# Layer 0's input projection computed by Strassen's seven block products instead of eight

## The chip, the cores and the metric

One core of a Trainium2 chip runs the whole program. The metric is the device time of one execution in microseconds (us). Three runs of the kernel before gave 2211.99, 2215.3 and 2217.59 us, a median of 2215.3 us.

## What is computed

The program is one inference step of a two-layer decoder trunk, for a prompt of 2048 tokens and 64 sample tokens (8 sequences of 8) that share the weights. Layer 0 runs a pooling mixer and a differential attention behind one joint input projection; layer 1 is gated linear attention (GLA). The change concerns the input projection of layer 0 and what uses its result:

```python
def even_layer(x, pos0, layer_idx, pool_buf, k_past, v_past,
               w_in, w_pool_lin, pool_scale, lam, subln_w, w_out, ln_g, ln_b):
    b, t, _ = x.shape
    pu, pg, q, k, v, ag = jnp.split(x @ w_in, EVEN_SPLITS, axis=-1)
    pool_out, new_buf = pool_mixer(pu, pool_buf, pos0, w_pool_lin, pool_scale)
    ...
    q = rope_partial(q.reshape(b, t, DA_HEADS, 2, DA_QK_DIM), pos) * DA_QK_DIM ** -0.5
    k = rope_partial(k.reshape(b, t, DA_HEADS, 2, DA_QK_DIM), pos)
    ...
    mix = jnp.concatenate([pool_out * jax.nn.silu(pg), o * jax.nn.silu(ag)], axis=-1)
    y = layer_norm(DN_ALPHA * x + mix @ w_out, ln_g, ln_b)
```

Here x has 2112 rows of 1024 and w_in has 3072 columns, six blocks of 512: the pool input pu and its gate pg, queries q, keys k, values v and the attention's gate ag. The pool mixer takes, for each of 4 groups of 128 channels, the mean over the last 2, 4, 8 or 16 tokens minus the token, maps it by a 128x128 matrix and scales it.

## The kernel before, in words

Every fp32 operand of the projection is cut in two: a high part (a cast to the fp32r type) and a low part (the raw value minus the high part). `split` (L39) does it: the cast on ScalarE (ACT, L42) or VectorE (DVE, L46), the subtraction on DVE (L47). A product is then three matmuls, high by high, high by low and low by high (`mm3`, L53 to L55), added up in one bank of PSUM.

`project_even` (L254) works in two halves. The first half is feature-major: the 2048 columns of queries, keys, pool inputs and pool gates are 16 blocks of 128, taken in 8 pairs by `fm_pair` (L274). A pair runs over five chunks of tokens (512, 512, 512, 256 and 320, the last with the 64 sample tokens), and each chunk is 8 slices of the contraction by 3 matmuls for each of its two blocks. In these matmuls (named pm<-xh,wh and so on) a 128x128 piece of the weights stands still and 512 tokens stream. The first pair is the rotated part of queries and keys (`rope_sink`), then four pairs of a pool group and its gate (`pool_sink`), then three pairs that are only copied out.

For a chunk of a pool group, ACT copies the input out of PSUM (ut, L349) and takes the gate's SiLU (sg, L352). DVE builds the trailing sums in one to four doublings (wp, L335), subtracts the token (dd, L355; the first 16 tokens anew, L358 and L359), cuts dd into dh and dl (L46, L47); TensorE (PE) multiplies by the group's matrix with three small matmuls (pl); DVE scales that and multiplies the gate (mx, L376). The two banks of the pool `pl` hold nothing but these products. While DVE does this for one chunk, PE does the 48 matmuls of the next.

The second half is token-major: for the gates (L427) and then the values (L440) 128 tokens stand still and 512 columns stream (pt<-wh,xh), 24 matmuls per tile of 128 tokens, 16 tiles, and one tile for the sample tokens. GpSimd (POOL) multiplies the gate by a weight (L428) and issues its store (L429). Among the last value tiles `layers` (L175) issues the first steps of the attention (`units`), and after that the attention's first head is woven with the pool half of the output projection (`out_pool`, names zp).

Weights come through a queue of SyncE (SP) as units of 128x1024 (L143), in raw buffers of which there are four, and are cut into four places for pairs of high and low parts (L144). All of x stays in SBUF as high and low parts (`XSplit`). A scheduler sets the order of the instructions on each engine from the program's text and buffers; each engine then works through its own list in that order.

Of the kernel before, what the change touches and what calls it, by code (L numbers as in the profile page):

```python
# [11 lines left out]
F32 = mybir.dt.float32  # L12
# [37 lines left out]
def mm3(nc, ps, lh, ll, rh, rl, n, first=True, last=True):  # L50

    for k in range(n):
        nc.tensor.matmul(ps, lh(k), rh(k), start=(first and k == 0), stop=False)  # L53
        nc.tensor.matmul(ps, lh(k), rl(k), start=False, stop=False)  # L54
        nc.tensor.matmul(ps, ll(k), rh(k), start=False, stop=(last and k == n - 1))  # L55
# [75 lines left out]

class Weights:
# [21 lines left out]
    def fm_pieces(self, src):  # L154

        nc = self.tc.nc
        hl = [self.place(self.i + 1 + j) for j in range(2)]
        self.i += 2

        def load(k):  # L160
            r = self.raw.tile([128, 2, 256], F32, name=f"wr{self.i}_{k}", **self.kw)
            ks = slice(128 * k, 128 * k + 256)
            nc.sync.dma_start(r, src[:, :, ks].rearrange("b p f -> p b f"))
            for j, (h, l) in enumerate(hl):
                split(nc, r[:, j, :], h[:, ks], l[:, ks], "dve" if j else "act")

        return [self.cut(h, l) for h, l in hl], load

# [6 lines left out]
def layers(tc, d):  # L175
# [4 lines left out]
    right, fill_banks, odd = ExitStack(), ExitStack(), ExitStack()  # L180
    with ExitStack() as left:
        raw = left.enter_context(tc.tile_pool(name="p0raw", bufs=4))
        wp = left.enter_context(tc.tile_pool(name="p0w", bufs=4))
# [7 lines left out]
        xs = {}  # L191

        def room(*names):
            for c in names:
                xs[c] = ExitStack()
                yield xs[c].enter_context(tc.tile_pool(name=f"p0x{c}", bufs=1, side="left" if c > 1 else "right"))

        x4, x3, x2 = room(4, 3, 2)
        tile_ = project_even(tc, d, raw, W, slot, psf, room, x2, x3, x4)
        for i in range(8):  # L200
            tile_(i)

        xs[0].close()

        keep = odd.enter_context(tc.tile_pool(name="keep", bufs=2, side="right", **rw))
        A = Attention(tc, d, right, psf, keep)
        A.load_k(0, 0)
        A.minus_lambda()
        A.load_q(0, 0)
        for i in range(8, 12):  # L210
            tile_(i)
        xs[2].close()
        A.room_weights()
        units = A.units([0], [1])
        for i in (12, 13):
            tile_(i)
            next(units)
        xs[3].close()
        A.room_values()
        A.load_v(0, 0)  # L220
        for i in (14, 15):
            tile_(i)
            next(units)
        tile_(16)
        xs[4].close()
        A.room_results()
        weave(units, out_pool(tc, d, A, W, slot), HEAD_COST, 17 * 8 * 640)
# [26 lines left out]
def project_even(tc, d, raw, W, slot, psf, room, x2, x3, x4):  # L254
# [3 lines left out]
    with ExitStack() as fm:  # L258
        x0, = room(0)
        ps = fm.enter_context(tc.tile_pool(name="p0ps", bufs=4, space=PSUM))  # L260
        pl = fm.enter_context(tc.tile_pool(name="p0pl", bufs=2, space=PSUM))
        wfm = d["w0_fm"]
        gw = x4.tile([128, 512], F32, name="gw")
        lh = x4.tile([128, 4, 128], F32R, name="lh")
        ll = x4.tile([128, 4, 128], F32R, name="ll")
        inv = x4.tile([128, 4, 16], F32, name="inv")
        X = XSplit(tc, [x0, x0, x2, x3, x4], [raw], d["xT"], "x")
# [3 lines left out]
        for c in range(1, 5):  # L271
            X.load(c)

# [1590 lines left out]
```

## Time and profile before

| what | value |
|---|---|
| time, median of 3 runs | 2215.3 us (2211.99 to 2217.59) |
| the profiled execution's own time | 2216.27 us |
| its span, first to last instruction | 2214.3 us |
| mean granted TensorE clock | 0.980 |
| PE busy | 2095.2 us, 95% of the span |
| DVE busy | 1140.4 us, 52% |
| ACT busy | 679.9 us, 31% |
| POOL busy | 654.4 us, 30% |
| first matmul of the projection | 6.79 us |

One line of the profile's groups gives the source line, the engine, the operation, the output and inputs by the program's names, the tile's shape and how many there were; behind the bar stand the busy time in us and the mean duration of one in ns, then the idle time of that engine ahead of these instructions with what ended it. A line of the timeline gives the start in us, the duration in us, and in brackets an idle time ahead of it with its releaser. PEld is PE's loading of the operand that stands still. A matmul's duration there is longer than the distance between two of them, since they overlap.

### The profile page before, as it was taken

The numbers are of one execution on the slowest core, as the hardware profiler recorded it, in microseconds if no ns is written. First come the engines' busy times: TensorE is split into PE (matmuls) and PEld (weight loads), VectorE is DVE, ScalarE is ACT, GpSimd is POOL, SyncE is SP. The second block draws the span as 40 slices with busy tenths as digits, with TensorE's granted clock in tenths as the row PEclk, the third lists the DMA queues.
The fourth block names the chain that finished last, engine by engine and source line by source line (L and its number), as shares of the span: only waits on it lengthen the run. The fifth ranks groups of instructions, "written<-read, shape, count | busy, mean of one in ns | idle before, by whom it ended". The sixth has DMA issues, their size and how long they took to land. (4 is left out here: it accounts for less than half of the span.)

```text
span 2214.3 us, 31442 instructions
## 1 busy us (share of the span) xinstructions
PE 2095.2 (95%) x11697; PEld 1751.9 (79%) x11697; DVE 1140.4 (52%) x2342; ACT 679.9 (31%) x1402; POOL 654.4 (30%) x698
## 2 busy tenths in 40 slices
PE   8999999999899999888988899999999997999997
PEld 7888888888688777667877688888888885887786
DVE  7445411012566676896678654810110127789984
ACT  2111000112433555655545311401111124333441
POOL 0000000322454433666443300000003342555654
PEclk9999999999999999899999999999999997999999
DMA  8411123125755598544222443311211246455521
GB/s 264 131 45 44 40 86 115 68 103 171 235 165 159 157 307 274 172 153 131 89 85 76 146 155 116 128 66 51 83 69 67 87 137 209 156 164 176 168 89 73
DMA packets 202595, 288.49 MB, mean 130 GB/s; under 512 B 30818, under 2 KB 121314, under 8 KB 202434
## 3 DMA queue, kind: packets, MB, share of 16 engines
q1 hardware_dynamic: 166594, 225.30, 32.8%
q0 software_dynamic: 12688, 43.00, 5.1%
q10 hardware_dynamic: 23152, 18.09, 2.5%
q8 instruction: 94, 1.54, 0.3%
q14 instruction: 67, 0.55, 0.1%
HBM read 183.95 MB, written 102.38 MB: 129 GB/s over the span
## 5 line engine op out<-in xcount | busy, mean ns | idle before, releaser
L53 PE MATMUL pm<-xh,wh 128*128 128x512 f32 (+2 forms) x640 | 224.5, 354 | 6.8 <-ACT xh L42 6.8
L54 PE MATMUL pm<-xl,wh 128*128 128x512 f32 (+2 forms) x640 | 226.4, 354 | 1.6 <-DVE xl L47 1.6
L55 PE MATMUL pm<-xh,wl 128*128 128x512 f32 (+2 forms) x640 | 225.8, 353 | 0.5 <-DVE wl L47 0.5
L614 ACT ACTIVATE e<-sc,nm 128x896 f32<-128x896 f32 (+10 forms) x192 | 164.9, 864 | 115.3 <-DVE nm L612 57.4
L55 PE MATMUL vt<-wk,yl 128*128 128x512 f32 x512 | 199.9, 391 | 0.0
L54 PE MATMUL vt<-wk,yh 128*128 128x512 f32 x512 | 199.7, 390 | 0.0
L53 PE MATMUL vt<-wk,yh 128*128 128x512 f32 x512 | 197.1, 391 | 0.0
L1099 POOL TENSOR_TENSOR ve<-ve,nw 128x512 f32<-128x512 f32 (+1 forms) x34 | 44.8, 1320 | 471.8 <-ACT ve L1098 471.7
L599 DVE TENSOR_REDUCE nm<-sc 128x1 f32<-128x768 f32 (+7 forms) x160 | 156.5, 991 | 29.3 <-PE sc L595 17.5
L594 PE MATMUL sc<-kst,qh 128*128 128x512 f32 (+9 forms) x352 | 135.1, 387 | 29.0 <-ACT e L614 24.8
L639 PE MATMUL po<-vt,aT 128*128 128x128 f32 x1088 | 153.4, 281 | 1.2 <-ACT aT L651 0.9
L428 POOL TENSOR_TENSOR et<-et,gw 128x512 f32<-128x512 f32 (+1 forms) x17 | 22.3, 1313 | 447.1 <-ACT et L427 447.1
L639 PEld LDWEIGHTS po<-vt,aT 128*128 128x128 f32 x1088 | 139.0, 195 | 9.4 <-issue 4.6
L46 DVE CAST wk<-wr 128x1024 fp32r<-128x1024 f32 x14 | 10.7, 768 | 251.3 <-PE vt L63 250.6
L53 PEld LDWEIGHTS pm<-xh,wh 128*128 128x128 f32 x640 | 120.9, 189 | 22.2 <-ACT xh L42 6.8
L54 PEld LDWEIGHTS pm<-xl,wh 128*128 128x128 f32 x640 | 121.0, 189 | 18.6 <-DVE xl L47 3.4
L55 PEld LDWEIGHTS pm<-xh,wl 128*128 128x128 f32 x640 | 121.1, 189 | 16.1 <-DVE wl L47 1.0
L595 PE MATMUL sc<-kst,ql 128*128 128x512 f32 (+9 forms) x352 | 123.2, 353 | 0.0
L53 PE MATMUL qm<-yh,wk 128*128 128x512 f32 (+2 forms) x320 | 114.0, 357 | 5.4 <-DVE yh L46 4.8
L651 ACT ACTIVATE aT<-tp 128x512 f32<-128x512 f32 (+3 forms) x160 | 85.5, 534 | 94.1 <-PE tp L646 92.5
L54 PE MATMUL qm<-yl,wk 128*128 128x512 f32 (+2 forms) x320 | 114.3, 357 | 0.0
L55 PE MATMUL qm<-yh,wk 128*128 128x512 f32 (+2 forms) x320 | 114.1, 356 | 0.0
(395 smaller groups left out, 5110.2 us busy)
## 6 DMA issues: line engine op xcount, KB each, us to landing
sk<-in_cachek SPq DMA_DIRECT2D x64, 256.0 KB
sv<-in_cachev SPq DMA_DIRECT2D x64, 256.0 KB
wr<-in_w_tm SPq DMA_DIRECT2D x24, 512.0 KB
wr<-in_w_fm SPq DMA_DIRECT2D x22, 512.0 KB
wr<-in_w_out SPq DMA_DIRECT2D x16, 512.0 KB
kr<-k SPq DMA_DIRECT2D x32, 256.0 KB
qr<-q SPq DMA_DIRECT2D x64, 128.0 KB
zx<-in_x SPq DMA_DIRECT2D x32, 256.0 KB
```

What stands on the lines that cost most here:

```text
L46: h = nc.vector.tensor_copy(hi, raw)
L53: nc.tensor.matmul(ps, lh(k), rh(k), start=(first and k == 0), stop=False)
L54: nc.tensor.matmul(ps, lh(k), rl(k), start=False, stop=False)
L55: nc.tensor.matmul(ps, ll(k), rh(k), start=False, stop=(last and k == n - 1))
L428: nc.gpsimd.tensor_tensor(out=e, in0=e, in1=gw[:n], op=ALU.mult)
L594: nc.tensor.matmul(o, qh[:, c, qs], kst[:, ks], start=True, stop=False)
L595: nc.tensor.matmul(o, ql[:, c, qs], kst[:, ks], start=False, stop=k < npc - 1)
L599: nc.vector.tensor_reduce(out=nm[:, c, i:i + 1], in_=p[:, :, :w], op=ALU.max, axis=AX.XY, negate=True)
L614: nc.scalar.activation(o, p, AF.Exp, bias=nm[:, m, 0:1], accum_out=s[:, m, i if npc > 1 else 0:][:, :1])
L639: nc.tensor.matmul(po, s[:, 128 * j:128 * j + 128], vt[:, k0 + j, :], start=(k0 + j == 0), stop=(k0 + j == n - 1))
L651: nc.scalar.activation(s[:, :128 * g], p[:, :128 * g], AF.Copy)
L1099: nc.gpsimd.tensor_tensor(out=e[:n], in0=e[:n], in1=nw[:n], op=ALU.mult)
```

## The change

The projection is done by a one-level Strassen scheme in Winograd's form. The 2048 prompt tokens are two sets of 1024, each of two halves of 512 (rows 1 and 2 of a 2x2 block matrix); the contraction is two halves of 512; the 3072 columns are three groups of 1024 (queries and keys; pool inputs and gates; attention gates and values), each of two halves. For each set and group, seven block products replace eight. With a11 to a22 the blocks of x and b11 to b22 those of w_in, the factors are s1 = a21 + a22, s2 = s1 - a11, s3 = a11 - a21, s4 = a12 - s2 on the side of x, and t1 = b12 - b11, t2 = b22 - t1, t3 = b22 - b12, t4 = b21 - t2 on the side of the weights. The products are run in the order 1, 2, 6, 7, 4, 5, 3: a11·b11, a12·b21, s2·t2, s3·t3, a22·t4, s1·t1, s4·b22. Each is four tiles of 12 matmuls of 512, that is 48 matmuls with two weight units.

Products 1, 6, 7 and 4 are added up one on another in the same four banks (`p`); product 2 has banks of its own (`q`, which are the pool `pl`, so product 2, the sample products and the pool mixes' small products take turns in two banks); products 5 and 3 are added up in `r`. ACT copies the running sum out after products 1, 6 and 7 (t, u, v); DVE adds product 2, 5 or 3 to one of the copies. Blocks 11, 21, 22 and 12 of the result are complete after products 2, 4, 5 and 3, in that order. So the four tiles of a pool group's second half of tokens come after product 5, those of its first half after product 3 (first-half inputs are there after product 2, but their gates only after product 3).

The sums of x are made by DVE for each set (`second`: six additions and four subtractions of low parts for each of four slices) and by POOL (`third`: three for each slice). The weight differences are made once for each group and kept in DRAM: those of the first group by DVE and POOL from the first weights loaded (`start`), those of the other two by POOL in 16 chunks of 256 columns (`make`), each with four loads on SP's queue into one set of buffers, four subtractions and four stores on POOL's queue. They are read back from there like other weights. The sample tokens, for which no such blocks exist, are multiplied by the plain blocks b11, b21, b12 - b11 and b22 in `SampleSide` (token-major, 8 matmuls with each of the four factors of a group, 96 in all; b12 - b11 is t1), and the feature-major results are transposed on PE. There are two raw weight buffers instead of four and three weight places instead of four. The attention's first steps are issued twice before the weave, instead of four times.

```diff
+PARTS = {1: ("a11", "b11"), 2: ("a12", "b21"), 3: ("s4", "b22"), 4: ("a22", "t4"), 5: ("s1", "t1"), 6: ("s2", "t2"),
+         7: ("s3", "t3")}
+ORDER = (1, 2, 6, 7, 4, 5, 3)
+CHAIN = {1: "p", 6: "p", 7: "p", 4: "p", 2: "q", 5: "r", 3: "r"}
...
+    def second(self, h):
...
+        for k in range(4):
+            ah, al = self.hi["a11"][:, k, :], self.lo["a11"][:, k, :]
+            r21, _ = self.fetch(h, "a21", k)
+            r22, load = self.fetch(h, "a22", k)
+            s2, s3 = (self.slot(f"{self.pre}{x}r{h}_{k}", 512) for x in ("s2", "s3"))
+            two(s3, ah, ALU.subtract, r21)
+            two(r21, r21, ALU.add, r22)
+            two(s2, r21, ALU.subtract, ah)
+            two(s2, s2, ALU.subtract, al)
+            self.cut("s2", k, s2)
+            two(s3, s3, ALU.add, al)
+            self.cut("s3", k, s3)
+            self.cut("a22", k, r22)
+            self.cut("s1", k, r21)
...
+    def third(self, h):
...
+            for x, y, op in ((hi["a12"][:, k, :], hi["s2"], ALU.subtract), (o, lo["s2"], ALU.subtract),
+                             (o, lo["a12"], ALU.add)):
+                nc.gpsimd.tensor_tensor(out=o, in0=x, in1=y[:, k, :], op=op)
+            self.cut("s4", k, o)
...
+    def done(m, j):
+        p = ps[CHAIN[m], j]
+        if m in (1, 6, 7):
+            t[m, j] = room({1: "t", 6: "u", 7: "v"}[m], j)
+            nc.scalar.activation(t[m, j], p, AF.Copy, scale=scale(j) if m == 1 else 1.0)
+        elif m == 4:
+            sink("21", j, p)
+        else:
+            o = t[{2: 1, 5: 7, 3: 6}[m], j]
...
+                nc.vector.tensor_tensor(out=o, in0=p, in1=o, op=ALU.add)
+            sink({2: "11", 5: "22", 3: "12"}[m], j, o)
...
+    def make(self, pool, groups, n=256):
...
+            for c in range(0, 2048, n):
+                b = []
+                for x in QUARTERS:
+                    b.append(pool.tile([128, n], F32, tag=x, name=f"{self.pre}m{x}{g}_{c}"))
+                    nc.sync.dma_start(b[-1], self.at(g, x)[:, c:c + n])
+                for x, v in differences(nc, *b, nc.gpsimd, nc.gpsimd).items():
+                    nc.gpsimd.dma_start(self.t[g][x][:, c:c + n], v)
+                yield
...
-        raw = left.enter_context(tc.tile_pool(name="p0raw", bufs=4))
-        wp = left.enter_context(tc.tile_pool(name="p0w", bufs=4))
+        raw = left.enter_context(tc.tile_pool(name="p0raw", bufs=2))
+        wp = left.enter_context(tc.tile_pool(name="p0w", bufs=3))
...
+        comb = own.enter_context(tc.tile_pool(name="p0m", bufs=1))
...
+        def start():
+
+            for k in range(4):
+                for x, v in differences(nc, *raw[k], nc.vector, nc.gpsimd).items():
+                    nc.gpsimd.dma_start(P.t[0][x][:, 512 * k:512 * k + 512], v)
+            X.third(0)
...
+        def run(gen, keep_up=True):
+            for i, _ in enumerate(gen):
+                if keep_up and i % 3 == 2:
+                    next(parts, None)
+
+        for h in range(2):
+            if h:
+                for gen in (X.first(1, ("a11", "a12")), X.second(1)):
+                    for _ in gen:
+                        pass
+                X.third(1)
```

What moves in the order of the instructions is shown at three places. The names are those of the program with a group and a chunk behind some: pl0_0 is the small product of pool group 0, chunk 0; f1_1 is tile 1 of a Strassen product; xs2 is the factor s2 of x.

The first place is PE's list where a pool group is mixed. Before, in the second pool chunk, the small product stands among the matmuls of a later chunk (pm2_1):

```order
L55 MATMUL pm2_1_760<-xh2_170,wl4_590 128x512
L53 MATMUL pm2_1_760<-xh2_170,wh4_589 128x512
L54 MATMUL pm2_1_760<-xl2_171,wh4_589 128x512
L53 MATMUL pl0_1_728<-dh0_1_724,lh_103 128x512
L55 MATMUL pm2_1_760<-xh2_170,wl4_590 128x512
L53 MATMUL pm2_1_760<-xh2_170,wh4_589 128x512
L54 MATMUL pl0_1_728<-dl0_1_725,lh_103 128x512
L55 MATMUL pl0_1_728<-dh0_1_724,ll_104 128x512
```

The three matmuls of the small product lie among those of the projection. Now, in the first set of tokens, behind the last tile of the next group's product 1 (f1_1<-wh30, the tile's last matmuls):

```order
L53 MATMUL f1_1_1813<-wh30_1808,xa11h0_150 128x512
L54 MATMUL f1_1_1813<-wl30_1809,xa11h0_150 128x512
L55 MATMUL f1_1_1813<-wh30_1808,xa11l0_151 128x512
L53 MATMUL pl3_1_1642<-dh3_1_1638,lin_1032 128x512
L54 MATMUL pl3_1_1642<-dl3_1_1639,lin_1032 128x512
L55 MATMUL pl3_1_1642<-dh3_1_1638,lin_1032 128x512
L53 MATMUL pl0_0_1703<-dh0_0_1699,lin_1032 128x512
L54 MATMUL pl0_0_1703<-dl0_0_1700,lin_1032 128x512
L55 MATMUL pl0_0_1703<-dh0_0_1699,lin_1032 128x512
L53 MATMUL pl1_0_1730<-dh1_0_1726,lin_1032 128x512
L54 MATMUL pl1_0_1730<-dl1_0_1727,lin_1032 128x512
L55 MATMUL pl1_0_1730<-dh1_0_1726,lin_1032 128x512
```

The small products of several tiles now follow each other with none of the projection's matmuls between them.

The second place is DVE's list at the same point. Before, a chunk of the second pool group:

```order
L335 TENSOR_TENSOR wp1_512_1_1094<-ut1_1_1089 128x526
L335 TENSOR_TENSOR wp1_512_2_1096<-wp1_512_1_1094 128x524
L355 SCALAR_TENSOR_TENSOR dd1_1_1098<-wp1_512_2_1096,ut1_1_1089 128x512
L46 CAST dh1_1_1100<-dd1_1_1098 128x512
L47 TENSOR_TENSOR dl1_1_1101<-dd1_1_1098,dh1_1_1100 128x512
L376 SCALAR_TENSOR_TENSOR mx1_1_1108<-pl1_1_1104,psc_578,sg1_1_1092 128x512
```

Now, in the first set, the fourth group's tile behind the third group's mx, and the weights of product 2's second half (wl32):

```order
L645 SCALAR_TENSOR_TENSOR mx2_0_1763<-pl2_0_1759,psc_101,u2_1287 128x512
L631 TENSOR_TENSOR wp03_1_1774<-t3_1123 128x526
L631 TENSOR_TENSOR wp03_2_1776<-wp03_1_1774 128x524
L631 TENSOR_TENSOR wp03_4_1778<-wp03_2_1776 128x520
L631 TENSOR_TENSOR wp03_8_1780<-wp03_4_1778 128x512
L653 SCALAR_TENSOR_TENSOR dd3_0_1782<-wp03_8_1780,t3_1123 128x512
L656 TENSOR_TENSOR dd3_0_1782<-wp03_8_1780,inv_285 128x16
L657 TENSOR_TENSOR dd3_0_1782<-dd3_0_1782,t3_1123 128x16
L46 CAST dh3_0_1786<-dd3_0_1782 128x512
L47 TENSOR_TENSOR dl3_0_1787<-dd3_0_1782,dh3_0_1786 128x512
L46 CAST wh32_1891<-wr32_1889 128x1024
L47 TENSOR_TENSOR wl32_1892<-wr32_1889,wh32_1891 128x1024
```

The rows of one tile are the same as before but stand in one block with those of the other tiles: each tile's rows stand behind the mx of the tile ahead, which needs PE's small product, and the weights of the next products stand behind the last tile's dl.

The third place is DVE's list between the first and the second set of tokens; the kernel before has nothing like it. Some ten of the 47 rows there:

```order
L47 TENSOR_TENSOR xs2l1_2399<-xs2r1_0_2410,xs2h1_2398 128x512
L185 TENSOR_TENSOR xs2r1_1_2429<-xa21r1_1_2425,xa11h1_2362 128x512
L47 TENSOR_TENSOR xs1l1_2405<-xa21r1_1_2425,xs1h1_2404 128x512
L47 TENSOR_TENSOR xs3l1_2401<-xs3r1_1_2430,xs3h1_2400 128x512
L185 TENSOR_TENSOR xs2r1_1_2429<-xs2r1_1_2429,xa11l1_2363 128x512
L185 TENSOR_TENSOR xs3r1_2_2449<-xa11h1_2362,xa21r1_2_2444 128x512
L47 TENSOR_TENSOR xa22l1_2403<-xa22r1_2_2446,xa22h1_2402 128x512
L185 TENSOR_TENSOR xa21r1_2_2444<-xa21r1_2_2444,xa22r1_2_2446 128x512
L185 TENSOR_TENSOR xs3r1_2_2449<-xs3r1_2_2449,xa11l1_2363 128x512
L47 TENSOR_TENSOR xs2l1_2399<-xs2r1_1_2429,xs2h1_2398 128x512
```

All four factors of a slice are made together, slice after slice, so the last piece of s2 (the factor of product 6) stands behind most of s3, a22 and s1.

More of the change, by code (lines that the diff above doesn't have):

```diff
@@ L477, in __init__ @@
         self.big = pool("aq", 1, side="right")
-        self.psc = pool("apsc", 2, space=PSUM)
-        self.ptp = pool("aptp", 1, space=PSUM)
-        self.pso = pool("apso", 1, space=PSUM)
+        self.psc = pool("apsc", 2, space=PSUM, side="right")
         self.psf = psf
```

594 lines of the change are left out of this document (404 added, 190 removed).

## The prediction

> **What bounds the kernel now.** The page's busy times and the table of 50-us stretches come first, to see which engine sets the pace of the projection and how far the others are from it.
>
> ```profile
> span 2214.3 us, 31442 instructions
> PE 2095.2 (95%) x11697; PEld 1751.9 (79%) x11697; DVE 1140.4 (52%) x2342; ACT 679.9 (31%) x1402; POOL 654.4 (30%) x698
> 0.00:50.00 50.00, 42.12 (x199) 34.75 (x200) 35.76 (x55) 13.85 (x17) 0.19 (x4) 1.00 0.83 267
> 200.00:250.00 50.00, 50.00 (x268) 43.89 (x267) 26.93 (x52) 5.65 (x10) 0.00 (x0) 1.00 0.14 41
> 300.00:350.00 50.00, 50.00 (x262) 43.59 (x261) 6.83 (x9) 3.68 (x6) 0.00 (x0) 1.00 0.32 97
> 400.00:450.00 50.00, 50.00 (x222) 41.42 (x221) 0.00 (x0) 5.39 (x9) 17.63 (x19) 1.00 0.12 48
> ```
>
> After the start PE is busy all the time in the projection, at a granted clock of 1.00. DVE is busy 26.93 of 50 us where pool groups are mixed, 6.83 where blocks are only copied, nothing among the gates. PE is the bound, and DVE has room only because its work is spread: the waits show it sitting idle for the small products of the pool mix.
>
> ```profile
> DVE mx L376 <- PE pl L55: 90.3, 17, 7.4
> L53 PE MATMUL pm<-xh,wh 128*128 128x512 f32 (+2 forms) x640 | 224.5, 354 | 6.8 <-ACT xh L42 6.8
> L54 PE MATMUL pm<-xl,wh 128*128 128x512 f32 (+2 forms) x640 | 226.4, 354 | 1.6 <-DVE xl L47 1.6
> L55 PE MATMUL pm<-xh,wl 128*128 128x512 f32 (+2 forms) x640 | 225.8, 353 | 0.5 <-DVE wl L47 0.5
> L53 PE MATMUL pt<-wh,xh 128*128 128x512 f32 x256 | 99.7, 390 | 0.0
> ```
>
> DVE waited 90.3 us for small products queued among PE's other matmuls. PE itself waited 6.8 us for the first x and 2.1 us more soon after. So fewer matmuls are time saved, as long as nothing else becomes the last to arrive.
>
> **What goes.** The stretch at 400 us holds nothing but matmuls of 512 columns: 222 in 50 us, 0.2253 us each. A pass pair is 240 matmuls (262 in 50 us, so 45.8 us), a pool pair 255 with its small products (268 in 50, so 47.6 us). The token-major half is 768 matmuls and 32 for the sample tokens. Together 4 x 47.6 + 4 x 45.8 + 800 x 0.2253 = 553.8 us. Afterwards there are 6 x 7 x 48 = 2016 matmuls of 512 and 96 for the sample tokens, 2112 x 0.2253 = 475.8 us, the small products (48 full ones and 12 of 64 columns, 11.5 us) and 16 small transposes (about 2): 489.3. **Gain: 64.5 us** if PE stays as full as it is.
>
> **What comes: DVE's price list.** The rows are from the first 580 us, one form each: the weights' low part and cast, the first doubling, dd, dl, dh, mx, and two subtractions or additions of 512.
>
> ```profile
> L47 DVE TENSOR_TENSOR wl<-wr,wh 128x1024 fp32r<-128x1024 f32 x25 | 31.3, 1261 | 7.8 <-ACT wh L42 7.3
> L46 DVE CAST wh<-wr 128x1024 fp32r<-128x1024 f32 x12 | 8.6, 719 | 95.6 <-PE pt L62 86.8 <-PE pm L54 6.3 <-DMA wr<-in_w_fm 1.8
> L335 DVE TENSOR_TENSOR wp<-ut 128x526 f32<-128x526 f32 x12 | 8.5, 706 | 1.1
> L355 DVE SCALAR_TENSOR_TENSOR dd<-wp,ut 128x512 f32<-128x512 f32 x12 | 8.3, 694 | 0.4
> L47 DVE TENSOR_TENSOR dl<-dd,dh 128x512 fp32r<-128x512 f32 x12 | 8.3, 692 | 0.4
> L46 DVE CAST dh<-dd 128x512 fp32r<-128x512 f32 x12 | 5.1, 428 | 0.4
> L376 DVE SCALAR_TENSOR_TENSOR mx<-pl,psc,sg 128x512 f32<-128x512 f32 x12 | 9.0, 751 | 63.5 <-PE pl L55 63.5
> L47 DVE TENSOR_TENSOR xl<-xr,xh 128x512 fp32r<-128x512 f32 x4 | 2.7, 686 | 0.0
> L300 DVE TENSOR_TENSOR ro<-ro,rt 128x512 f32<-128x512 f32 x3 | 2.1, 684 | 0.0
> ```
>
> And the timeline of one mix, to see that dependent steps follow each other without overlap:
>
> ```profile
> 221.58 0.69 DVE L355 SCALAR_TENSOR_TENSOR dd<-wp,ut 128x512 f32<-128x512 f32 x1
> 222.31 0.17 DVE L358 TENSOR_TENSOR dd<-wp,inv 128x16 f32<-128x16 f32 x1
> 222.52 0.18 DVE L359 TENSOR_TENSOR dd<-dd,ut 128x16 f32<-128x16 f32 x1
> 222.73 0.43 DVE L46 CAST dh<-dd 128x512 fp32r<-128x512 f32 x1
> 223.19 0.69 DVE L47 TENSOR_TENSOR dl<-dd,dh 128x512 fp32r<-128x512 f32 x1
> ```
>
> Starts lie 0.03 us beyond each duration. A whole mix with its small product (3 x 0.2253 on PE) is thus 0.72 + 0.46 + 0.72 + 0.68 + 0.78 = 3.4 us and 0.73 for each doubling: 4.1, 4.8, 5.6 and 6.3 us for windows of 2, 4, 8 and 16, and 0.4 more in the first chunk. Before, each lay under 48 matmuls, 10.8 us. Now four tiles are complete at the end of product 5 and four at the end of product 3, 41.6 us of DVE work in a set against 10.8 us between them, and DVE's list has the next products' weights behind them.
>
> *Pool group, first set (21 us).* After product 3's last addition DVE has, in its order: one weight low part (1.29), the end of one mix (3.4), a mix of window 16 (6.7 with two copies), the first chunk's mixes of 4.5, 5.2 and 6.0, the fourth's up to its dl (5.2), then a weight cast and two low parts (3.3). That is 35.6 us until product 6 has its first weights; product 2 can't step in, since its banks are those of the small products and its weights stand at that same place. PE has product 1, six small products and eight sample matmuls: (48 + 18 + 8) x 0.2253 = 16.7 us. It stands still for 19 us, and about 2 more go at the clock:
>
> ```profile
> 588.43 0.79 PE L53 MATMUL zp<-wh,zh 128*128 128x512 f32 x1 [7.30 <-ACT zh L42]
> 589.45 0.63 PE L53 MATMUL zp<-wh,zh 128*128 128x512 f32 x1
> 589.88 0.63 PE L54 MATMUL zp<-wl,zh 128*128 128x512 f32 x1
> 592.62 0.39 PE L53 MATMUL zp<-wh,zh 128*128 128x512 f32 x1
> 592.85 0.39 PE L54 MATMUL zp<-wl,zh 128*128 128x512 f32 x1
> ```
>
> After an idle time of 7.30 us the matmuls started 0.43 us apart, by 592.62 0.23: some 3.5 us at half speed, 1.7 us lost. The Trainium skill ("TensorE: Matmul & The Clock Gate", section "HAM oscillation — how this bites in real kernels") says that every gap longer than about 3.4 us sends the clock back; by it the small products, each behind such a gap and waited for by DVE, would all run at half speed, which would make this place and the next 4 us dearer each; the rows above agree with the mechanism.
>
> *Pool group, second set (20 us).* Its mixes divide. Between products 5 and 3 DVE has the second chunk's four mixes and the weights of product 3's second half: some 26 us, for 18 + 12 + 24 + 16 matmuls, 15.8 us on PE: 9 lost, with the wait between. After product 3 come the sample mixes (33 small operations and 4 round trips to PE, some 9 us by the 0.17 rows), four mixes (21), six weight operations (7) and additions (4): 41 us, against products 1 and 2, half of 6 and the small products, 30 us: 11 lost.
>
> *Between the sets (15 us).* DVE has 41 operations of 512 (0.66 with neighbours that overlap), four weight low parts and two casts, 34 us, ahead of the last piece of s2. PE has 104 matmuls, 23.4 us. That leaves 11, and Pool's share:
>
> ```profile
> 550.66 1.46 DVE L623 SCALAR_TENSOR_TENSOR e<-e,c,e 128x128 f32<-128x128 f32 x1
> 550.68 1.29 POOL L47 TENSOR_TENSOR ql<-qr,qh 128x512 fp32r<-128x512 f32 x1
> 552.68 0.48 DVE L623 SCALAR_TENSOR_TENSOR e<-e,c,e 128x256 f32<-128x256 f32 x1
> ```
>
> An operation on 128 columns beside Pool's 1.29 us took 1.46 us; on 256 columns alone it took 0.48. So the two take turns. Pool makes six to nine of s4's subtractions there, 8 to 12 us; I take 4, since Pool can be the one that waits. The Trainium skill ("SBUF — State Buffer", section "Who interferes with whom") has it as a rule: a DVE instruction with two SBUF inputs contends with a GpSimd one that reads SBUF, and the second to start is blocked altogether; with Pool always first, this place and the start would each be about 6 us dearer.
>
> *Start (22 us).* Before, PE has lost about 10.9 us when it is at speed: 6.8 and 2.1 waiting, and some 2 at half clock (as behind 588 us, above).
>
> ```profile
> 0.74 0.45 SPq L163 DMA_DIRECT2D wr<-in_w_fm  x1
> 1.25 0.45 SPq L96 DMA_DIRECT2D xr<-in_xT  x1
> 6.79 1.22 PE L53 MATMUL pm<-xh,wh 128*128 128x512 f32 x2 [6.79 <-ACT xh L42]
> L428 POOL TENSOR_TENSOR et<-et,gw 128x512 f32<-128x512 f32 x16 | 20.6, 1285 | 442.6 <-ACT et L427 442.6
> L429 POOL DMA_DIRECT2D sg<-et x17 | 10.1, 592 | 5.1 <-POOL et L428 5.1
> ```
>
> Products 1 and 2 need 16 loads of 256 KB; at 267 GB/s that is 15.7 us, the last landing near 19 us, and their 21.6 us of matmuls end near 30. Product 6 needs t2, through DRAM, and s2. From its first weight difference near 20 us DVE has 51 operations of 512 (0.62 to 0.69 each) and 3.3 us of weights before t2's second half is cut: 35 to 38 us, so 55 to 58; the eight subtractions on Pool (1.29 each) add 4 more. Product 6 ends 5.4 us later, near 65, with 144 matmuls (32.4 us) done. That is 32.6 lost, 22 more than before.
>
> *Differences of the other groups (4 us; 0 to 30).* 16 chunks at four subtractions of 256 columns (about half of 1.285 us) and four issues of 0.592 us: some 5 us of Pool each, with a load ahead of it and a store behind, one set of buffers; 8 to 11 us each, some 150 us in all, under two groups of 76 us. It just fits.
>
> *End (6 us; 0 to 12).* Two steps of the attention fewer are under way when the projection ends, and the wait of 7.30 us at 588 us grows; the units of the output projection are cut behind the last sums.
>
> ACT gets 72 copies of sums out of PSUM, of the kind that it made before for the same tiles; it is busy at most 13.85 us in any of the stretches above, so PE's matmuls hide them.
>
> **Sum.** 2216.3 (the profiled execution) - 64.5 + 22 + 21 + 15 + 20 + 4 + 6 = 2239.8. The median of the runs is 1.0 lower: **2239 us**.
>
> **Rivals.** *DVE's blocks don't bind (faster).* If the tiles of a pool group were mixed while PE has work, because DVE runs rows closer together or PE's tiles come spread, the three places cost nothing: 2216.3 - 64.5 + 22 + 4 + 6 = 2184, 2183 as a median. It decides at the three places whether PE has matmuls for 35 us. For it: DVE idles 23 of 50 us in the pool stretch before. Against: in the new order nothing but small products stands between two mixes. *Half of it.* If overlap takes half of the three places' 56 us, the result is 2211: no change. *The differences arrive late (slower still).* With Pool and DVE taking turns, or SP's queue held by the chunks' loads ahead of weight units, 16 chunks at 13 us don't fit under two groups, and each late weight is a stall: 30 us more, 2269. That the change doesn't do what it says is excluded by the count, 2016 for 2304.
>
> **Numbers.** The forecast has 0.53, the late differences 0.12, half 0.15, no binding 0.20. About 0.3% (6.6 us) is what a measurement can tell from no change: slower 0.65, same 0.15, faster 0.20. The forecast's own range is 2220 to 2260, from 0 to 12 at the end, Pool's turns and the start's 35 to 38; with the half case and the late differences, 2198 to 2270.
>
> **What would show it.** The projection's last matmul before, in the timeline:
>
> ```profile
> 572.85 0.40 PE L63 MATMUL pt<-wl,xs 128*128 128x512 f32 x1
> ```
>
> Right: product 6's first matmuls end near 65 us; PE idle in three or four places with mx, xs2l and weight low parts as releasers, a granted clock below 1 there, DVE near 100% at these places; about 490 us of projection matmuls; the projection's end near 590 us where it was 573. Wrong: PE full between 70 and 560 us (the first rival), or waits on weights' DMA or on Pool's stores (the third).

## The result and the profile after

The changed kernel takes 2338.0 us (median of 4 runs, 2332.0 to 2346.1) against 2216.5 us before: a ratio of 1.055, 95% interval 1.052 to 1.059. It is 122 us slower where 24 were forecast, and lies outside the range. The profiled execution is the longest of the four (2346.1 us), so lengths read from its trace stand some 8 us, in all, above the median. Its page begins:

```profile
span 2344.2 us, 31162 instructions
PE 2082.0 (89%) x11105; PEld 1704.8 (73%) x11105; DVE 1361.0 (58%) x2545; ACT 770.9 (33%) x1537; POOL 810.9 (35%) x876
```

PE has less work, and the execution is longer. The six stages of the projection (two sets of tokens by three column groups, each cut at the end of its last matmul on xs4, product 3) show where. In each row of the table of stretches stand the stretch, its length, the busy time of PE, PE's weight loads, DVE, ACT and POOL with their counts, the granted clock, the DMA engines' share and GB/s:

```profile
0.00:129.40 129.40, 86.42 (x337) 69.12 (x338) 96.33 (x102) 36.42 (x56) 64.77 (x76) 0.85 0.64 212
129.40:233.50 104.10, 82.38 (x344) 66.84 (x343) 47.41 (x61) 20.52 (x28) 52.96 (x73) 0.90 0.63 200
233.50:357.60 124.10, 99.23 (x387) 76.74 (x386) 68.77 (x94) 25.63 (x38) 34.58 (x40) 0.85 0.46 154
357.60:468.50 110.90, 93.53 (x373) 73.28 (x372) 70.08 (x90) 30.50 (x48) 19.36 (x12) 0.91 0.47 152
468.50:578.90 110.40, 93.55 (x389) 74.93 (x388) 55.75 (x87) 21.91 (x33) 0.00 (x0) 0.91 0.36 111
578.90:700.60 121.70, 93.60 (x393) 73.47 (x392) 69.38 (x121) 41.62 (x71) 35.11 (x36) 0.89 0.58 161
```

A stage's 336 matmuls need 75.7 us at 0.2253 us each; with the sample tokens' and the small products, 76 to 87. Every stage lasts 104 to 129 us, and in none is the clock whole. The projection ends at 700.6 us instead of 573; what follows lasts 1643.6 us against 1641, as before. So the whole loss lies in the projection.

The six stages last 53, 27, 37, 28, 25 and some 42 us longer than their matmuls need, 211 us in all against the forecast's 489 us of matmuls. PE's busy time in the six rows adds up to 548.7 us. So of the 211 us, 152 are idle time of PE, and at most 59 are matmuls that ran slowly. What PE waited for there:

```profile
PE pl L53 <- DVE dh L46: 45.3, 12, 6.8
PE f L53 <- ACT wh L42: 40.2, 2, 23.3
PE f L53 <- DVE wh L46: 19.5, 5, 6.4
PE f L53 <- ACT xs2h L42: 8.8, 3, 4.0
PE st L603 <- DVE sbo L69: 7.9, 1, 7.9
PE f L53 <- ACT xa11h L42: 6.5, 1, 6.5
PE f L53 <- ACT u L240: 6.4, 1, 6.4
PE f L54 <- DVE xs2l L47: 5.4, 3, 3.3
```

The first row is the pool mix, as forecast: some 30 us of it for the prompt's tiles and 15 for the sample tokens'. The second and third, 60 us, are weights whose cast came late; 34 of them stand in the first stage (23.3, 6.4 and 4.6), and for the others the forecast had 4 us. The rows add up to 140 of the 152 us of idle time.

Three places in the timeline show how. At the start, weight difference t2 comes back from DRAM late: SP's queue holds three stores of q ahead of its load, and these wait for DVE's sums, the first for 18.1 us (the first row is of the queue's own waits, in the first 60 us):

```profile
SPq L578 <- DVE t L246: 19.9, 3, 18.1
...
40.78 3.67 SPq L578 DMA_DIRECT2D q<-t  x3
44.56 1.48 SPq L379 DMA_DIRECT2D wr<-pt  x1
...
52.66 1.06 ACT L42 ACTIVATE wh<-wr 128x1024 fp32r<-128x1024 f32 x1 [2.88 <-DMA wr<-pt]
...
53.77 0.79 PE L53 MATMUL f<-xs2h,wh 128*128 128x512 f32 x1 [23.29 <-ACT wh L42]
```

DVE is slow there because Pool works beside it. These rows are the same timeline, DVE's and Pool's:

```profile
44.43 0.68 DVE L185 TENSOR_TENSOR xs3r<-xa11h,xa21r 128x512 f32<-128x512 f32 x1
46.26 1.72 DVE L185 TENSOR_TENSOR xa21r<-xa21r,xa22r 128x512 f32<-128x512 f32 x1
50.71 2.97 DVE L185 TENSOR_TENSOR xs2r<-xa21r,xa11h 128x512 f32<-128x512 f32 x1
...
45.87 1.56 POOL L324 TENSOR_TENSOR b<-b,b 128x512 f32<-128x512 f32 x1 [1.47 <-DVE b L323]
50.23 2.90 POOL L212 TENSOR_TENSOR xs4r<-xa12h,xs2h 128x512 f32<-128x512 f32 x2
```

An addition or subtraction on 512 columns takes 0.68 us alone, 1.72 beside one subtraction on Pool and 2.97 beside two. It isn't only these: a cast of weights, which has a single input, took 7.42 us while Pool subtracted almost without a pause, and PE waited for it. The 41 casts of this form in the projection have a mean of 955 ns; in the kernel `dve_sub` below, without Pool's subtractions, 734.

```profile
74.10 7.42 DVE L46 CAST wh<-wr 128x1024 fp32r<-128x1024 f32 x1 [1.73 <-DMA wr<-pt]
74.73 3.77 POOL L212 TENSOR_TENSOR xs4r<-xs4r,xa12l 128x512 f32<-128x512 f32 x3
...
81.57 0.50 PE L53 MATMUL f<-xs3h,wh 128*128 128x512 f32 x1 [4.59 <-DVE wh L46]
```

Third, the first set's pool group: product 2's weights stand on SP's queue behind a row of 27 issues that begins at 128.07 us, 19 of them stores of the first stage's queries and keys and seven loads of chunks (pmb; the last of them is shown), and PE waits 16.88 us. Later in this stage the queue is held by the chunks' loads themselves: they waited 46.6 us for stores out of the same buffers (first row, the queue's own waits in the second stage).

```profile
SPq L362 <- DMA pt<-pmb: 46.6, 21, 6.0
...
150.77 0.84 SPq L362 DMA_DIRECT2D pmb<-in_w_q  x1
151.71 0.93 SPq L379 DMA_DIRECT2D wr<-in_w_q  x2
...
158.10 1.06 ACT L42 ACTIVATE wh<-wr 128x1024 fp32r<-128x1024 f32 x1 [15.13 <-DMA wr<-in_w_q]
...
159.21 0.80 PE L53 MATMUL f<-xa12h,wh 128*128 128x512 f32 x1 [16.88 <-ACT wh L42]
```

### The profile page after: what moved, and what is told of

Its sections match the earlier page's. It is cut to its first block, busy times and chain, and to the rows that moved or that the text cites. A ratio compares the mean times of both kernels' runs of the same rounds, so it can differ in the third digit from the quotient of the medians.

```text
span 2344.2 us, 31162 instructions
## 1 busy us (share of the span) xinstructions
PE 2082.0 (89%) x11105; PEld 1704.8 (73%) x11105; DVE 1361.0 (58%) x2545; ACT 770.9 (33%) x1537; POOL 810.9 (35%) x876
## 5 line engine op out<-in xcount | busy, mean ns | idle before, releaser
L47 DVE TENSOR_TENSOR wl<-wr,wh 128x1024 fp32r<-128x1024 f32 x92 | 122.7, 1337 | 72.3 <-ACT wh L42 69.9
L53 PE MATMUL qm<-yh,wk 128*128 128x512 f32 (+2 forms) x320 | 114.3, 358 | 5.4 <-DVE yh L46 4.8
L42 ACT ACTIVATE wh<-wr 128x1024 fp32r<-128x1024 f32 x46 | 48.7, 1059 | 192.2 <-PE f L54 51.0
L54 PEld LDWEIGHTS vt<-wk,yh 128*128 128x128 f32 x512 | 96.2, 188 | 20.6
L55 PEld LDWEIGHTS vt<-wk,yl 128*128 128x128 f32 x512 | 96.2, 188 | 20.5
L53 PEld LDWEIGHTS vt<-wk,yh 128*128 128x128 f32 x512 | 96.2, 188 | 20.4
L946 PEld LDWEIGHTS sc<-kst,qh 128*128 128x128 f32 x352 | 69.4, 197 | 55.9 <-ACT e L966 48.4
L998 PE MATMUL tp<-ident,e 128*128 128x128 f32 x544 | 91.8, 284 | 12.3 <-ACT aT L1003 4.9
```

What stands on the lines that cost most here:

```text
L42: h = nc.scalar.activation(hi, raw, AF.Copy)
L47: return h, (lo_eng or nc.vector).tensor_tensor(out=lo, in0=raw, in1=hi, op=ALU.subtract)
L54: nc.tensor.matmul(ps, lh(k), rl(k), start=False, stop=False, **kw)
L946: nc.tensor.matmul(o, qh[:, c, qs], kst[:, ks], start=True, stop=False)
L998: nc.tensor.transpose(p[:, 128 * j:128 * j + 128], a[:, 128 * (k0 + j):128 * (k0 + j) + 128], self.ident)
```

## The experiments

**Theory A**: the difference chain of the weights (Pool's subtractions, which hold DVE up, its loads and stores on the queues) costs most of what the forecast lacks. **Theory B**: DVE's own list is longer than forecast. The kernels are compared with the changed kernel's 2338.0 us; its runs spread over 14 us, so single runs that differ by less than about 8 us are taken as equal. All but `best` are single runs. The kernel before took 2214.2 to 2217.9 us beside them. Stage lengths are read from each trace at the same marks. What follows the six stages is the same program in all of them and lasts 1630.8 to 1645.7 us, so some us of a difference in the whole time can come from there, and the stages say more than the total.

| kernel | us | stage 1 | 2 | 3 | 4 | 5 | 6 |
|---|---|---|---|---|---|---|---|
| changed | 2338.0 | 129.4 | 104.1 | 124.1 | 110.9 | 110.4 | 121.7 |
| no_make | 2297.7 | 114.3 | 85.0 | 114.2 | 112.5 | 112.3 | 120.1 |
| no_diff | 2283.3 | 106.9 | 85.1 | 114.2 | 110.2 | 111.1 | 119.8 |
| dve_sub | 2328.0 | 126.7 | 100.6 | 114.8 | 110.0 | 111.4 | 123.4 |
| no_mix | 2283.8 | 127.7 | 103.4 | 98.3 | 111.6 | 96.6 | 113.6 |
| queues | 2316.7 | 116.3 | 99.3 | 117.9 | 101.4 | 111.4 | 122.8 |
| s2_first | 2337.1 | 127.2 | 103.6 | 121.8 | 109.3 | 111.6 | 122.9 |
| no_x | 2304.5 | 115.0 | 96.8 | 122.3 | 93.3 | 112.7 | 123.9 |
| no_sub | 2316.6 | 115.9 | 105.8 | 114.0 | 111.2 | 111.8 | 121.5 |
| sample | 2316.4 | 127.7 | 105.3 | 126.6 | 104.4 | 107.2 | 99.1 |
| best | 2286.6 | 118.5 | 94.3 | 119.2 | 93.6 | 109.4 | 102.9 |
| bare | 2189.7 | 88.3 | 82.6 | 83.2 | 91.9 | 97.3 | 108.6 |
| bare_sample | 2165.3 | 88.1 | 81.8 | 83.2 | 90.4 | 94.8 | 88.4 |

### The difference chain left out: no_make and no_diff

```diff
+        if g and x[0] == "t":
+            x = {"t1": "b11", "t2": "b22", "t3": "b12", "t4": "b21"}[x]
         return self.src[g, QUARTERS.index(x)] if x[0] == "b" else self.t[g][x]
...
-        parts = P.make(comb, (1, 2))
+        parts = iter(())
```

> Leaves out the differences of the second and third column group (their loads, Pool's subtractions and the stores) and reads the plain weight blocks b11, b22, b12, b21 in place of t1 to t4 there, so these groups' results are other numbers with the same amount of work on PE. Theory A (Pool's difference chain: its subtractions block DVE's two-input operations, and its loads hold SP's queue ahead of weight units): the first set's pool group loses its 28 us of standstill and the start some 10 us, so about 2338 - 40 = 2298 us. Theory B (DVE's own list is too long, Pool's part is the 4 us of the forecast): about 2334 us.

2297.7 us, 40 less: theory A's number, though not by its parts (28 us in stage 2 and 10 at the start were expected). Stage 2 became 19 us shorter, the start 15 and stage 3 ten. But 40 us isn't most of the 98 that the forecast lacks. The second kernel takes the first group's differences out as well (the condition without `g and`, and `start` with only `X.third(0)`):

> As the run before it, and the first group's differences are left out too, with plain blocks read in their place: nothing is stored to DRAM and read back, DVE and Pool have 16 subtractions less at the start; s4 stays on Pool. Theory A: PE's loss at the start falls from 54 us to about 25, the whole comes to about 2275 us. Theory B: DVE has 8 operations less, 6 us, and what the missing round trip through DRAM gives: about 2320 us.

2283.3 us, 14 less again, of which 7 in stage 1; nearer to theory A (2275) than to B (2320). PE's loss at the start fell from 54 to 31 us, so the differences account for 22.5 of it.

### Subtractions or queues: no_sub, queues, dve_sub

```diff
-                for x, v in differences(nc, *b, nc.gpsimd, nc.gpsimd).items():
+                for x, v in zip(("t2", "t3", "t4", "t1"), (b[3], b[1], b[2], b[0])):
```

> Leaves out only Pool's 64 subtractions of the chunks of the second and third group: the loads on SP's queue, the stores on Pool's queue and the reading back stay (plain blocks are stored in place of t1 to t4). Leaving out the whole chain took 40 us off. If the subtractions (Pool's time and the lock that they hold against DVE) are the cost: most of that, about 2305 us. If the queues are (loads and stores that weight units stand behind): little, about 2328 us.

2316.6 us, midway between the two expectations: 21 of the chain's 40 us go with Pool's subtractions, the other 19 with the loads, stores and queues. They act in different stages: without the subtractions the start and stage 3 shrink as in no_make, while stage 2 stays at 105.8.

```diff
-                    nc.sync.dma_start(b[-1], self.at(g, x)[:, c:c + n])
+                    nc.gpsimd.dma_start(b[-1], self.at(g, x)[:, c:c + n])
...
-            nc.sync.dma_start(d["v0"][t0:t0 + n, :], e)
-            nc.sync.dma_start(d["newv"][t0:t0 + n, :], e)
+            nc.gpsimd.dma_start(d["v0"][t0:t0 + n, :], e)
+            nc.gpsimd.dma_start(d["newv"][t0:t0 + n, :], e)
```

> Same results. The loads of the difference chunks (64) and the stores of values go out on Pool's queue instead of SP's. If SP's queue is what makes weight units late (a chunk's load that waits for its buffer stands ahead of them, and value stores stand ahead of the second set's x): the first set's pool group goes from 104 us to about 90 and the second set's queries and keys from 111 to about 105, about 2318 us in all. If it is the lock between Pool and DVE: no gain, and Pool has 64 issues of 0.57 us more, about 2345 us.

2316.7 us, the queue theory's total, though by other stages than expected, so that the agreement is in part luck: the start gave 13 us, stage 4 nine and a half (101.4; about 105 was expected), stage 2 only five (99.3; about 90 was expected). In stage 2 the stores of queries and keys still stand ahead of product 2's weights (PE waits 11.64 us for them), and t2 then comes late (5.62 us), since its load waits 15.6 us for the store of a difference. So the order on the queue explains a quarter of the 19 us that this stage gains without the chain. What makes up the rest stays open; the DMA engines' share there is 0.63 in the changed kernel and 0.40 in no_make, and whether this traffic by itself delays the weights wasn't tried.

```diff
-                for x, v in differences(nc, *b, nc.gpsimd, nc.gpsimd).items():
+                for x, v in differences(nc, *b, nc.vector, nc.vector).items():
...
-                for x, v in differences(nc, *raw[k], nc.vector, nc.gpsimd).items():
+                for x, v in differences(nc, *raw[k], nc.vector, nc.vector).items():
...
-                nc.gpsimd.tensor_tensor(out=o, in0=x, in1=y[:, k, :], op=op)
+                nc.vector.tensor_tensor(out=o, in0=x, in1=y[:, k, :], op=op)
```

> All subtractions of Pool in the projection (64 of 256 columns and 8 of 512 for the weights, 24 of 512 for s4) are done by DVE: 50 us more of DVE work (64 x 0.43 + 32 x 0.69), the same results. Theory A in its form that the lock between Pool and DVE is the cost: Pool's subtractions held DVE up for at least as long as DVE itself takes for them, so the time falls by 20 to 40 us, about 2308 us. Theory B (DVE's amount of work): up to 50 us slower, about 2375 us.

2328.0 us, between the two and just beyond the changed kernel's spread. DVE took over some 50 us of work and the kernel did not get slower. DVE's busy time in the six stages is 407.7 us in the changed kernel, for 551 instructions, and 407.3 here, for 649. Pool's subtractions had been costing DVE about as much as doing them itself (the third busy time of these rows, the changed kernel's first):

```profile
0.00:700.60 700.60, 548.71 (x2217) 434.38 (x2217) 407.70 (x551) 176.60 (x273) 206.77 (x236) 0.88 0.52 165
0.00:686.90 686.90, 554.66 (x2218) 437.57 (x2219) 407.32 (x649) 176.84 (x274) 101.29 (x141) 0.88 0.54 169
```

The groups show it too. In the changed kernel, two of the operations on x, then in the kernel `best` below, which has no subtraction on Pool:

```profile
L47 DVE TENSOR_TENSOR xs2l<-xs2r,xs2h 128x512 fp32r<-128x512 f32 x8 | 9.0, 1121 | 0.8 <-ACT xs2h L42 0.7
L185 DVE TENSOR_TENSOR xs2r<-xa21r,xa11h 128x512 f32<-128x512 f32 x8 | 8.8, 1103 | 0.0
```

```profile
L47 DVE TENSOR_TENSOR xs2l<-xs2r,xs2h 128x512 fp32r<-128x512 f32 x8 | 5.5, 688 | 0.0
L185 DVE TENSOR_TENSOR xs2r<-xa21r,xa11h 128x512 f32<-128x512 f32 x8 | 5.5, 687 | 0.0
```

1121 and 1103 ns became 688 and 687. This agrees with the rule that the prediction cites from the Trainium skill ("SBUF — State Buffer", section "Who interferes with whom"): with two SBUF inputs on DVE and a Pool operation that reads SBUF, one waits for all of the other.

### The pool mix: no_mix

```diff
         def pool_mix(g, c, ut, sg, lin):
...
+            m = slot(f"mx{g}_{c}", 512)
+            nc.vector.tensor_tensor(out=m, in0=ut[:, 15:527], in1=sg, op=ALU.mult)
+            nc.sync.dma_start(d["mixp"][g, :, 512 * c:512 * c + 512], m)
```

> Leaves out the pool mix of the prompt's tiles but for one multiplication (no windows, no dd, no cuts, no small products, 16 tiles), so y is another result; DVE loses 16 x 2.7 to 4.9 us, PE 48 small matmuls (10.8 us). If the two pool places cost what the forecast said (21 + 20 us, and 11 of PE): about 2338 - 52 = 2286 us. If they cost what the trace shows (36 + 57 us lost in the four stages that hold the mixes, of which some 15 is weights): about 2250 us.

2283.8 us, 54 less, beside 52 from the forecast's price and 88 from reading all losses of those stages as the mix's. The stages that hold the mixes became 25.8, 13.8 and 8.1 us shorter. With PE's 11 us shared equally, the first set's price is met (26 forecast, 25.8 measured). The second set's 25 had the sample mixes in it, which stay in this kernel; without them 21.9 were measured. In the changed kernel's timeline, PE's small products of the first set:

```profile
256.00 0.55 PE L53 MATMUL pl<-dh,lin 128*128 128x512 f32 x1 [2.77 <-DVE dh L46]
261.69 0.80 PE L53 MATMUL pl<-dh,lin 128*128 128x512 f32 x1 [3.34 <-DVE dh L46]
267.44 0.79 PE L53 MATMUL pl<-dh,lin 128*128 128x512 f32 x1 [3.81 <-DVE dh L46]
273.94 0.79 PE L53 MATMUL pl<-dh,lin 128*128 128x512 f32 x1 [4.54 <-DVE dh L46]
281.15 0.79 PE L53 MATMUL pl<-dh,lin 128*128 128x512 f32 x1 [5.27 <-DVE dh L46]
```

They stand 5.7 to 7.2 us apart, the forecast's 4.5, 5.2, 6.0 and 6.7 us for these mixes and half a microsecond to 1.2 more; from the second on the matmul is at half clock (0.79 us for 0.39).

### The sums of x: s2_first and no_x

```diff
-                for gen in (X.first(1, ("a11", "a12")), X.second(1)):
+                for gen in (X.first(1, ("a11", "a12")), X.second_s2(1)):
```

where `second_s2` makes s2 of all slices in one loop and the other factors in a second one.

> Same results. In the second set DVE makes all four slices of s2 first and then s3, a22 and s1 (a21 and a22 are loaded twice, four additions more). If the length of DVE's list ahead of the last piece of s2 sets the standstill between the sets: some 20 operations of 0.69 us fewer stand ahead of it, the second set's queries and keys fall from 111 us to about 98, 2325 us in all. If the loads of x (slots and SP's queue) set it: no change, or some us slower by the eight loads more.

2337.1 us: no change, stage 4 became 1.6 us shorter. The new order did what it was meant to do: the low part of the last piece of s2 is ready 34.7 us after the stage's start instead of 48.3. But PE then waited for something else. The first row is the changed kernel's, the others are this kernel's (its fourth stage starts at 352.6 us, the changed kernel's at 357.6):

```profile
405.21 0.69 DVE L47 TENSOR_TENSOR xs2l<-xs2r,xs2h 128x512 fp32r<-128x512 f32 x1 [0.70 <-ACT xs2h L42]
...
386.66 0.68 DVE L47 TENSOR_TENSOR xs2l<-xa21r,xs2h 128x512 fp32r<-128x512 f32 x1
...
371.88 0.80 PE L324 MATMUL sax<-wh,xs 128*128 128x512 f32 x1 [5.63 <-DVE wh L46]
385.08 0.77 PE L53 MATMUL f<-xs2h,wh 128*128 128x512 f32 x1 [3.72 <-DVE wh L46]
404.91 0.79 PE L53 MATMUL f<-xs3h,wh 128*128 128x512 f32 x1 [5.41 <-ACT wh L42]
```

In the changed kernel PE's waits for pieces of s2 add up to 14.2 us (8.8 and 5.4 in the table of waits), about the forecast's 15. Here waits for weights, whose casts stand in DVE's and ACT's lists among the same work, took their place. So the order alone gains nothing; that the list's length does not matter isn't shown, and the eight loads and four additions that this kernel has more blur the test. The list was also longer than the forecast had it: in that stage the changed kernel's DVE stood idle for x (1.77, 3.46, 0.68 and 1.90 us), and five of its operations took 1.75 to 1.77 us beside Pool.

```diff
-            two(s3, ah, ALU.subtract, r21)
-            two(r21, r21, ALU.add, r22)
-            two(s2, r21, ALU.subtract, ah)
-            two(s2, s2, ALU.subtract, al)
-            self.cut("s2", k, s2)
-            two(s3, s3, ALU.add, al)
-            self.cut("s3", k, s3)
+            self.cut("s2", k, r21)
+            self.cut("s3", k, r22)
...
-            for x, y, op in ((hi["a12"][:, k, :], hi["s2"], ALU.subtract), (o, lo["s2"], ALU.subtract),
-                             (o, lo["a12"], ALU.add)):
-                nc.gpsimd.tensor_tensor(out=o, in0=x, in1=y[:, k, :], op=op)
+            o, _ = self.fetch(h, "a12", k)
```

> Leaves out the sums and differences of x: s2 and s1 are plain a21, s3 and a22 plain a22, s4 plain a12 (loaded again), so the results are other numbers; cuts and matmuls stay. DVE has 24 operations of 512 fewer in each set, Pool 24 in all. If DVE's and Pool's work on x sets the standstills at the start and between the sets: the first stage falls from 129 us to about 112 and the fourth from 111 to about 92, 2302 us in all. If the weights' round trip sets the start: the first stage stays near 125.

2304.5 us, as expected: 14 less at the start, 18 in stage 4. The amount of work on x counts (DVE's and Pool's together); the order in which DVE does it gained nothing by itself. The kernel leaves out 20 of DVE's operations in each set, not 24: `second` makes five additions and subtractions for each slice, beside the four of low parts, and not six as the description of the change has it.

### The sample side: sample

```diff
-            self.done(0, self.sum(self.p, 0))
+            self.o = self.sum(self.p, 0)
+        elif (m, before) == (2, False):
+            self.done(0, self.o)
...
         def sample_pool(lin):
+            uss = []
+            for g, x in enumerate(QUARTERS):
+                uss.append(comb.tile([128, 256], F32, tag=x, name=f"us{g}")[:, :184].rearrange("p (n t) -> p n t", n=8))
+                nc.sync.dma_start(uss[g][:, :, 0:15], d["state_pool"][g])
...
-                    us = slot(f"us{g}", 184).rearrange("p (n t) -> p n t", n=8)
-                    nc.sync.dma_start(us[:, :, 0:15], d["state_pool"][g])
+                    us = uss[g]
```

> Same results. The state rows of the four sample pool mixes are loaded one group of products ahead, into tiles that are free by then, and the sample results' transposes stand behind the next product's matmuls instead of ahead of them. If PE's waits there (8 us for the sum, 7 and 6 us for the small products of 64 columns, with the slow clock behind each) are lost time: about 20 us less, 2318 us, all of it in the fifth and sixth stage. If the pool mixes of the prompt hold these stages anyway: under 8 us.

2316.4 us, 22 less, in stages 4 to 6. The waits that went are these, in the changed kernel's timeline:

```profile
492.53 0.68 PE L603 MATMUL st<-ident,sbo 64*128 64x64 f32 x4 [7.95 <-DVE sbo L69]
...
605.28 0.42 PE L53 MATMUL pl<-dh,lin 128*128 128x64 f32 x1 [6.84 <-DVE dh L46]
...
612.53 0.42 PE L53 MATMUL pl<-dh,lin 128*128 128x64 f32 x1 [6.36 <-DVE dh L46]
```

Behind the last two stood a load each, as the waits name it:

```profile
DVE ws L631 <- DMA us<-in_state_pool: 17.0, 4, 4.8
```

### Together, and with all of it left out: best, bare, bare_sample

`best` joins queues, dve_sub and sample; it leaves nothing out.

> Same results. Together: chunk loads and value stores on Pool's queue, all subtractions on DVE, state rows loaded ahead and the transposes behind the product. If the gains add (21 + 10 + 20): about 2287 us. If the first two are one and the same cost: about 2297 us. Still slower than the kernel before by some 70 us, since the pool mixes and the sums of x stay.

2286.6 us (median of 4 runs, 2283.8 to 2291.5), a ratio to the kernel before of 1.032, interval 1.030 to 1.034. The gains add (21, 10 and 22 make 53; 51 measured), and it is still slower than before. Stage 4 is down to 93.6 us with a clock of 0.96, stage 3 with its mixes hardly moved:

```profile
212.80:332.00 119.20, 97.33 (x387) 75.77 (x387) 67.71 (x98) 25.86 (x38) 27.79 (x37) 0.87 0.46 143
332.00:425.60 93.60, 88.42 (x374) 71.19 (x373) 67.94 (x101) 29.73 (x47) 2.25 (x5) 0.96 0.53 179
```

`bare` joins no_diff, no_mix and no_x.

> Leaves out the weight differences, the sums of x and the prompt's pool mix together (as in the three kernels that leave out one each). What stays is the 2112 matmuls, the cuts, the copies out of PSUM and their sums, and the sample tokens. If the added work on DVE and Pool is the whole loss: stages of about 85, 77, 84, 84, 84 and 85 us, the projection ends near 500 us and the whole comes to about 2338 - 200 = 2140 us. If two raw buffers and three weight places are too few by themselves: weight waits remain, 2170 us or more.

2189.7 us, 25 less than the kernel before beside it, and 50 more than the 2140 expected if the added work were the whole loss. Stages 5 and 6 still had 97 and 109 us. With the sample side's edit as well:

> As the kernel that leaves out the differences, the sums of x and the prompt's pool mix, and with the sample rows loaded ahead and the transposes behind the product. If the added work and the sample side are all that stands between PE and its gain: 64.5 us of matmuls saved and 10.8 us of small products left out, some 2216 - 75 + 10 = 2150 us. If the gains of the two only add: 2190 - 22 = 2168 us. Near 2190 us: the sample side cost nothing where nothing else is late.

2165.3 us, 52 less than the kernel before beside it (2217.5). The gains add once more (2168 expected for that), and 24 of the 50 us were the sample side. The stretch of stage 2 (which lasts from 88.1 to 169.9 us) without the added work:

```profile
87.00:170.00 83.00, 79.34 (x344) 65.26 (x343) 35.65 (x56) 22.20 (x32) 0.00 (x0) 0.98 0.47 152
```

So most of the matmuls saved are saved in time: of 64.5 us, and 10.8 of small products left out, 52 arrive. The rest lies in stages of 82 to 95 us where 76 to 83 are work, among them PE's waits for weights (5.9 us in two) and for a sum (4.0). Whether two raw buffers and three weight places are the cause of these wasn't tried.

## Why the prediction was wrong

The direction and the gain on PE were right, and the pool mix of the prompt was priced about right. The other terms were too small. By stages, the forecast had some 33, 0, 21, 15, 9 and 11 us beyond the matmuls, and 4 for the differences; measured were 53, 27, 37, 28, 25 and 42.

- **"Differences of the other groups (4 us; 0 to 30)"** is the step that failed most: 40 us, 15 of them at the start and 19 in the second stage, where the forecast had nothing. It asked only whether 16 chunks fit in time under two groups ("it just fits"). It did not ask what else stands behind them: their loads and stores, and SP's queue, which holds them ahead of weight units (19 us together), and Pool's subtractions, which stop DVE in the stages where PE waits for DVE (21 us). The third rival, with a chance of 0.12 and 30 us, named both and was nearly the size of this term, but it sat beside the forecast instead of in it, and its total of 2269 us was 69 short as well.
- **"Start (22 us)"** measured 43 more than before (54 lost against 11). The first group's round trip and the other groups' chunks together account for 22.5 of the 54, the sums of x for 14. The working priced DVE's 51 operations at 0.62 to 0.69 us, where 1.2 to 1.9 was common, and left out that t2's load stands behind three stores of q that wait for DVE.
- **"Between the sets (15 us)"** measured 28 in stage 4 (110.9 against 83 of work): 17 of idle time and some 11 of slow matmuls, for which the working had nothing here. Its mechanism is in the trace: PE waited 14.2 us for pieces of s2. But the last piece was ready after 48 us and not 34, and it wasn't the only thing late: when it came 14 us sooner, weights were late instead. Late loads of x behind value stores (queues: 9.5 us), Pool's share and the sample side's transposes (6.5) had a part in the 28 us.
- **"Pool group, second set (20 us)"** counted the sample mixes as DVE work. What they cost was PE's waits for loads and for a sum, 22 us with those of the queries and keys. (Its first part, 26 us of DVE less 15.8 of PE, makes 10 and not 9.)
- **The clock** was counted as 2 us at one place. The granted clock is 0.85 to 0.91 in all six stages, and the matmuls behind the waits quoted above ran at half speed. By PE's busy time slow matmuls are at most 59 of the 211 us. How much of that is loss of its own, rather than hidden under DVE's pace, the runs don't tell. The dearer small products, which the prediction names as a possibility beside its sum, are there (0.79 us), but the mixes came to their price all the same.
- **"End (6 us)"** measured about 3 (1643.6 us after the projection for 1641), less than this part differs from kernel to kernel.

## What to carry to other kernels

Fewer matmuls are worth their time only where the engines that prepare operands have room in the same stage; list what the saving adds there per stage, and add each engine's work to what already stands in its order. Work on Pool isn't free beside DVE: count a Pool subtraction in DVE's time too, unless the two never meet. Of every added load or store, ask which transfer stands behind it on its queue, and who waits for that one. When several things are late at the same place, taking one away shows only the next: s2_first brought its factor 14 us sooner and gained nothing.

## What the runs showed of the hardware

A DVE operation with two SBUF inputs that took 0.68 us alone took 1.72 and 2.97 us beside one and two subtractions on Pool; without them the mean of eight such operations fell from 1121 to 688 ns. A cast on DVE, with one SBUF input, took 7.42 us beside a row of Pool's subtractions. Six stages of waits of 1 to 23 us held the mean granted clock of the projection at 0.85 to 0.91, where it had been 1.00.
